# A transformer block stack on one core: the convolved x of the state-space mixer returns to token layout through 32x32 squares and DRAM instead of TensorE transposes, and the decay tiles are loaded later

## The chip, the cores and the metric

The kernel runs on one core of a Trainium2 chip. TensorE multiplies matrices, VectorE and ScalarE work element by element, GpSimd does very little here, and SyncE (SP) issues most of the transfers; ScalarE issues some on a queue of its own. Each engine works through its own instructions in a fixed order and stops at one whose inputs are not ready. The metric is device time in microseconds (us).

## What is computed

The input is 256 tokens of 2048 numbers. The first block is a hybrid mixer (a Mamba-2 style state-space branch, "SSD", and gated linear attention) with an MLP; two attention layers follow. Everything is float32. The change lies in the SSD branch:

```
z, xbc, dt, ... = split(h @ w_in)
xbc = silu(conv4(xbc) + b)                 # 4096 channels of x, 1024 of B, 1024 of C
x   = xbc's x as (256 tokens, 64 heads, 64)        # 8 groups g of 8 heads
xdt = x * dt
y_diag = einsum(cb * decay, xdt)           # decay = exp(masked differences of cumsum(dt*A))
states = einsum(B, xdt * exp(a_last - a_cs))
y   = y_diag + C @ states_before * exp(a_cs) + D * x
y   = grouped_rms_norm(y * silu(z)) ; branch = y @ w_ssd_branch
```

## The kernel before

**Products.** Each weight block of 128x1024 is a unit. SP loads it (`stage`, L128, tile `ws`, five buffers), ScalarE casts it to a rounded high part (L136, `wh`), VectorE subtracts to get the low part (L137, `wl`; five buffers each), and TensorE does three products per matrix (L141 high by high, L142 low by high, L143 high by low), twelve matmuls per unit. A unit can be cast only when TensorE has finished the unit five places ahead.

**Order.** `drive()` walks through the units; after every second unit it steps the generators ("posts") that treat finished products. The order on each engine is then settled by a scheduler when the program is built. `yield` marks where a post can be interrupted.

**One group of SSD.** For each of eight groups there are a product for x (512 channels), one for z, and from the third group on products of the w_ssd branch. `x_post` (L586) loads two decay tiles `E` of 128x1024 (one per half of the tokens) from `acs_rows` in DRAM, convolves, and then needs x by tokens: eight 128x128 transposes on TensorE (L603) into PSUM, multiplied by VectorE (L604 `xdt`, L607 `xw`, L609 `y`). ScalarE turns E into decays (eight relus L613 and one exp L615 per half), VectorE multiplies by `cbm` (L616). TensorE then does `st` (L620, copied by ScalarE at L622), `y` (L626, eight matmuls per half) and `yo` (L632). `z_post` (L638) multiplies y by silu(z), normalizes it and calls `to_op_t` (L359, L362), which makes the operand `yT` of the w_ssd branch.

**Turning through DRAM.** The convolution and `to_op_t` already use `turn`: VectorE transposes 32x32 squares (L328), ScalarE's queue writes them to a DRAM tile in four transfers of 128 KB (L334), and SP reads it back as one of 512 KB into `tn` (L337). SP and ScalarE stop in that order until the data is there. The DRAM tile `turn` has four buffers.

Of the kernel before, what the change touches and what calls it, by code (L numbers as in the profile page):

```python
# [13 lines left out]
ALU = mybir.AluOpType  # L14
# [3 lines left out]
P = 128  # L18
# [3 lines left out]
NB = 512  # L22
# [6 lines left out]
Z0, XBC0, DT0, Q0, K0, V0, G0, LR0, GS0, GG0 = (  # L29
    0, 4096, 10240, 10304, 11328, 12352, 14400, 16448, 16464, 18512)  # L30
# [23 lines left out]
W_IN_COLS = (  # L54
    [XBC0 + 4096 + 512 * i for i in range(4)]
    + [c for g in range(8) for c in (XBC0 + 512 * g, Z0 + 512 * g)]
    + [GS0 + 512 * i for i in range(4)]
    + [V0, V0 + 512, Q0, K0, V0 + 1024, V0 + 1536, Q0 + 512, K0 + 512]
    + [G0 + 512 * i for i in range(4)]
    + [GG0 + 512 * i for i in range(4)]  # L60
)
# [17 lines left out]
def tile_blocks(ctx, tc, a, out):  # L79
    nc = tc.nc  # L80
# [11 lines left out]
    def nm(s):  # L92
        uid[0] += 1
        return f"{s}_{uid[0]}"

    def t4(shape, dt=F32, s="t4"):
        return tpool.tile(shape, dt, tag="t4", name=nm(s))
# [4 lines left out]
    def small(shape, s="sm"):  # L102
        return spool.tile(shape, F32, tag="sm", name=nm(s))
# [4 lines left out]
    def aux(shape, s="aux"):  # L108
        return psa.tile(shape, F32, tag="aux", name=nm(s))
# [212 lines left out]
    def turn(src, got):  # L322

        sq = t4([P, 4, 4, 2, 32], s="sq")
        for m in range(2):
            V.transpose(sq[:, :, :, m, :].rearrange("p b c i -> p c b i"),  # L328
                        src[m].rearrange("p (c b j) -> p c b j", c=4, b=4))
        d = dram.tile([P, 1024], F32, tag="turn", name=nm("turn"), bufs=4)  # L330
        sv = sq.rearrange("p b c m i -> p (b c m i)")
        dv = d.rearrange("(b j) (q r) -> q j b r", b=4, q=4)
        for q in range(4):
            S.dma_start(dv[q], sv[32 * q:32 * q + 32, :].rearrange("j (b r) -> j b r", b=4))  # L334
        yield
        tn = t4([P, 4, 4, 2, 32], s="tn")
        nc.sync.dma_start(tn.rearrange("p q c m i -> p (q c m i)"), d)  # L337
        got.append(tn)
        yield
# [91 lines left out]
    ident = cst[:, C_ID:C_ID + P]  # L431
# [149 lines left out]
    def heads8(ap):  # L581
        return ap.rearrange("p (h d) -> p h d", h=8)
# [2 lines left out]

    def x_post(g, need):  # L586
        def post(ps):
            es = [t4([P, 8, P], s="E") for _ in range(2)]
            for m in range(2):
                nc.sync.dma_start(es[m], acs_rows[g, m].partition_broadcast(P))  # L590
            xc = t4([P, 4, T], s="xc")
            yield from conv_silu(ps, 4 * g, xc)
            for h in need:
                while not h[0].done:
                    yield
            hs = slice(8 * g, 8 * g + 8)
            y = ys[g] = t4([P, 2, 512], s="y")
            xdt = t4([P, 2, 512], s="xdt")
            xw = small([P, 512], "xw")
            for m in range(2):  # L600
                pt = aux([P, 512], "tr")
                for f in range(4):
                    nc.tensor.transpose(pt[:, f * P:f * P + P], xc[:, f, m * P:m * P + P], ident)  # L603
                V.tensor_tensor(heads8(xdt[:, m, :]), heads8(pt),  # L604
                                dt[:, m, hs].unsqueeze(2).to_broadcast([P, 8, 64]), op=ALU.mult)
                if m == 0:
                    V.tensor_tensor(heads8(xw), heads8(pt),  # L607
                                    dtw[:, hs].unsqueeze(2).to_broadcast([P, 8, 64]), op=ALU.mult)
                V.tensor_tensor(heads8(y[:, m, :]), heads8(pt),  # L609
                                Dbc[:, hs].unsqueeze(2).to_broadcast([P, 8, 64]), op=ALU.mult)  # L610
                e = es[m]
                for h in range(8):
                    S.activation(e[:, h, :], e[:, h, :], AF.Relu, scale=-1.0,  # L613
                                 bias=acs[:, m, 8 * g + h:8 * g + h + 1])
                S.activation(e, e, AF.Exp, scale=-1.0)  # L615
                V.tensor_tensor(e, e, cbm[m][:, g, :].unsqueeze(1).to_broadcast([P, 8, P]), op=ALU.mult)  # L616
                yield

            ps = aux([P, 512], "st")
            nc.tensor.matmul(ps, Btok[:, g, :], xw, start=True, stop=True)  # L620
            st = small([P, 512], "st")
            S.copy(st, ps)  # L622
            for m in range(2):
                py = aux([P, 512], "y")
                for h in range(8):
                    nc.tensor.matmul(py[:, h * 64:h * 64 + 64], es[m][:, h, :], xdt[:, m, h * 64:h * 64 + 64],  # L626
                                     start=True, stop=True)
                V.tensor_tensor(y[:, m, :], y[:, m, :], py, op=ALU.add)
                if m == 0:
                    yield  # L630
            po = aux([P, 512], "yo")
            nc.tensor.matmul(po, CT1[:, g, :], st, start=True, stop=True)  # L632
            yo = small([P, 512], "yo")
            V.tensor_tensor(heads8(yo), heads8(po), ea1[:, hs].unsqueeze(2).to_broadcast([P, 8, 64]),
                            op=ALU.mult)
            V.tensor_tensor(y[:, 1, :], y[:, 1, :], yo, op=ALU.add)
        return post
# [828 lines left out]
def _blocks(w, kcs=4, n=NB):  # L1466

    k, c = w.shape
    v = w.reshape(k // (kcs * P), kcs, P, c // n, n)
    return np.ascontiguousarray(v.transpose(3, 0, 2, 1, 4)).reshape(-1, P, kcs * n)  # L1470
# [29 lines left out]
def _vec(v):  # L1500

    return np.asarray(v).reshape(-1, P).T


def _bias(rpb):

    t = np.arange(T)
    r, c = t // 64, t % 64
    c0 = np.clip(c - 8, 0, 48)
    q, k = t[:, None], t[None, :]  # L1510
    inside = (c[k] >= c0[q]) & (c[k] < c0[q] + 16)
    dr = r[k] - r[q] + 7
    dc = np.where(inside, c[k] - c[q] + 15, 0)
    out = np.full((2, 4, T, T), -1e30, np.float32)
    out[:, :, inside] = rpb[:, :, dr, dc][:, :, inside]
    return np.ascontiguousarray(out.reshape(2, 4, 2, P, T).transpose(0, 1, 3, 2, 4)).reshape(2, 4, P, -1)


def _layout(x):
# [2 lines left out]
    o["x"] = a["x"][0]  # L1522
    o["xT"] = np.ascontiguousarray(a["x"][0].T.reshape(16, P, T).transpose(1, 0, 2)).reshape(P, 16 * T)
    o["consts"] = _consts()
    cw = a["ssd_conv_w"][0]
    o["vec"] = np.ascontiguousarray(np.concatenate(
        [_vec(cw[j]) for j in range(4)]
        + [_vec(a["ssd_conv_b"][0]), _vec(a["ssd_norm_w"][0]), _vec(a["gla_norm_w"][0]),
           _vec(a["ln1_g"][0]), _vec(a["ln1_b"][0]),
           _vec(a["ln2_g"][0]), _vec(a["ln2_b"][0]), _vec(a["norm_pre_2"][0]), _vec(a["norm_pre_2"][1]),  # L1530
           _vec(a["b_q_norm_2"][0]), _vec(a["b_q_norm_2"][1]), _vec(a["b_kv_norm_2"][0]),
           _vec(a["b_kv_norm_2"][1])], axis=1))
    w = a["w_in"][0]
    o["w_in"] = np.concatenate([_blocks(w[:, c:c + NB]) for c in W_IN_COLS])
    o["w_dtlr"] = _blocks(np.concatenate([w[:, LR0:LR0 + 16], w[:, DT0:DT0 + 64]], axis=1), 16, 80)[0]
    o["gk_w"] = np.concatenate([a["gla_gk_w"][0], a["gla_gk_b"]], axis=0)
    o["w_ssd"] = _blocks(a["w_ssd_branch"][0])
# [36 lines left out]
```

## Time and profile before

| | us |
|---|---|
| median of 3 runs | 2867.42 (2863.65 to 2869.07) |
| the profiled execution | 2869.14 |
| its span, first to last instruction | 2867.4 |
| TensorE busy in the span | 2835.7 (99%) |
| VectorE busy | 1816.3 (63%) |
| ScalarE busy | 1428.6 (50%) |

The granted TensorE clock averages 0.998 of full speed. The transfers move 603 MB, 210 GB/s over the span. The eight SSD groups lie between about 140 and 650 us. In a row of a timeline the first number is the start and the second the length, both in us; in square brackets stands how long the engine was idle before, and what released it. Engine names with a q (ACTq, SPq) are instructions that only issue a transfer. Lengths of matmuls overlap, so the pitch is read from their starts.

### The profile page before, as it was taken

What the parts mean: (1) busy time and instruction counts of PE and PEld (TensorE: products, weight loads), DVE (VectorE), ACT (ScalarE), POOL (GpSimd) and SP (SyncE); (2) the same over time, 40 slices, a digit from 0 to 9 for tenths busy, and PEclk for the clock granted to TensorE, in tenths of its full rate; (3) what the DMA queues carried; (4) which work ended last, traced back from release to release, by engine and by line L of the source; (5) the groups of instructions that cost most, each with busy time, mean ns of one, the idle gap of its engine ahead of it and who ended that gap; (6) DMA issues with size and microseconds to landing.
All of it is one profiled execution on the core that took longest, in us unless ns stands there. A gap on an engine that the chain in (4) does not pass through costs nothing.

```text
span 2867.4 us, 35163 instructions
## 1 busy us (share of the span) xinstructions
PE 2835.7 (99%) x13040; PEld 2343.8 (82%) x13040; DVE 1816.3 (63%) x2357; ACT 1428.6 (50%) x2013; POOL 37.8 (1%) x49
## 2 busy tenths in 40 slices
PE   9999999999999999999999999999999999999998
PEld 7787888888887878887888888888788888798887
DVE  6777677775844845665666555555776555666564
ACT  5565655554444544444444443444565544655543
POOL 0000000000000000000000000000000000000000
PEclk9999999999999999999999999999999999999999
DMA  8766666666664656675676666667466676466674
GB/s 287 220 218 216 220 221 220 221 221 214 189 183 141 216 159 224 216 270 163 218 233 223 222 213 216 210 223 253 149 199 221 195 233 221 147 212 215 215 236 140
DMA packets 199759, 603.15 MB, mean 210 GB/s; under 512 B 22545, under 2 KB 56721, under 8 KB 199586
## 3 DMA queue, kind: packets, MB, share of 16 engines
q1 hardware_dynamic: 161858, 566.27, 60.9%
q10 hardware_dynamic: 37728, 34.62, 3.9%
q8 instruction: 102, 1.67, 0.2%
q14 instruction: 71, 0.58, 0.1%
HBM read 564.56 MB, written 36.24 MB: 210 GB/s over the span
## 4 chain that ended last, share of the span: by engine, by line
PE 84%; DMA 7%; DVE 4%; ACT 2%; issue 1%; ACTq 1%; SPq 0%; DVEq 0%; POOL 0%; POOLq 0%
PE mm L141 26%; PE mm L142 26%; PE mm L143 26%; DMA turn<-sq 3%; DVE wl L137 2%; PE sc L1107 1%; DMA tn<-turn 1%; PE po L1139 1%; DMA ws<-in_w_in 1%; ACT wh L136 1%; DMA E<-acs_rows 1%; ACTq L334 1%; PE y L626 1%; PE tr L272 1%; ACT E L613 0%
## 5 line engine op out<-in xcount | busy, mean ns | idle before, releaser
L137 DVE TENSOR_TENSOR wl<-ws,wh 128x1024 fp32r<-128x1024 f32 (+2 forms) x974 | 1170.4, 1211 | 773.9 <-ACT wh L136 767.8
L136 ACT CAST wh<-ws 128x1024 fp32r<-128x1024 f32 (+2 forms) x974 | 1007.3, 1044 | 1006.6 <-PE mm L143 864.2
L141 PE MATMUL mm<-wh,xh 128*128 128x512 f32 x1280 | 503.9, 395 | 1.5 <-DVE xh L419 1.0
L142 PE MATMUL mm<-wl,xh 128*128 128x512 f32 x1280 | 499.1, 390 | 2.5 <-DVE wl L137 2.5
L143 PE MATMUL mm<-wh,xl 128*128 128x512 f32 x1280 | 499.0, 390 | 0.0
L141 PE MATMUL mm<-wh,lnh 128*128 128x512 f32 (+1 forms) x896 | 344.6, 388 | 6.0 <-ACT lnh L304 6.0
L142 PE MATMUL mm<-wl,lnh 128*128 128x512 f32 (+1 forms) x896 | 347.1, 387 | 0.0
L143 PE MATMUL mm<-wh,lnl 128*128 128x512 f32 (+1 forms) x896 | 346.4, 387 | 0.0
L141 PEld LDWEIGHTS mm<-wh,xh 128*128 128x128 f32 x1280 | 240.5, 188 | 56.8 <-issue 3.9
L142 PEld LDWEIGHTS mm<-wl,xh 128*128 128x128 f32 x1280 | 240.5, 188 | 55.9 <-DVE wl L137 4.5
L143 PEld LDWEIGHTS mm<-wh,xl 128*128 128x128 f32 x1280 | 240.3, 188 | 50.4 <-DVE xl L420 0.2
L141 PEld LDWEIGHTS mm<-wh,lnh 128*128 128x128 f32 x896 | 168.2, 188 | 40.2 <-ACT lnh L304 7.0
L142 PE MATMUL mm<-wl,hT 128*128 128x512 f32 x512 | 199.4, 389 | 0.5 <-DVE wl L137 0.5
L143 PE MATMUL mm<-wh,hT 128*128 128x512 f32 x512 | 199.2, 389 | 0.0
L141 PE MATMUL mm<-wh,hT 128*128 128x512 f32 x512 | 199.2, 389 | 0.0
L143 PEld LDWEIGHTS mm<-wh,lnl 128*128 128x128 f32 x896 | 168.2, 188 | 34.1 <-DVE lnl L305 0.9
L142 PEld LDWEIGHTS mm<-wl,lnh 128*128 128x128 f32 x896 | 168.2, 188 | 33.6 <-DVE wl L137 0.4
L141 PE MATMUL mm<-wh,hh 128*128 128x512 f32 (+1 forms) x384 | 147.7, 386 | 3.7 <-ACT hh L304 3.7
L142 PE MATMUL mm<-wl,hh 128*128 128x512 f32 (+1 forms) x384 | 148.0, 385 | 0.2 <-DVE wl L137 0.2
L143 PE MATMUL mm<-wh,hl 128*128 128x512 f32 (+1 forms) x384 | 147.3, 384 | 0.4 <-DVE hl L305 0.4
L142 PEld LDWEIGHTS mm<-wl,hT 128*128 128x128 f32 x512 | 96.1, 188 | 21.1 <-DVE wl L137 1.2
L141 PEld LDWEIGHTS mm<-wh,hT 128*128 128x128 f32 x512 | 96.1, 188 | 20.0
(371 smaller groups left out, 3408.3 us busy)
## 6 DMA issues: line engine op xcount, KB each, us to landing
ws<-in_w_in SPq DMA_DIRECT2D x494, 512.0 KB
ws<-in_w_up SPq DMA_DIRECT2D x128, 512.0 KB
ws<-in_w_down SPq DMA_DIRECT2D x128, 512.0 KB
ws<-in_w_out SPq DMA_DIRECT2D x96, 512.0 KB
turn<-sq ACTq DMA_DIRECT2D x260, 128.0 KB
tn<-turn SPq DMA_DIRECT2D x65, 512.0 KB
ws<-in_w_ssd SPq DMA_DIRECT2D x64, 512.0 KB
ws<-in_w_gla SPq DMA_DIRECT2D x32, 512.0 KB
```

Of the source, the lines that this page charges most:

```text
L136: S.copy(hi[:, c], st[:, c])
L137: V.tensor_tensor(lo[:, c], st[:, c], f32(hi[:, c]), op=ALU.subtract)
L141: nc.tensor.matmul(ps, l[0], r[0], start=first, stop=False)
L142: nc.tensor.matmul(ps, l[0], r[1], start=False, stop=False)
L143: nc.tensor.matmul(ps, l[1], r[0], start=False, stop=last)
L272: nc.tensor.transpose(dst[:, i, m * P:m * P + P], src[:, m, (ft + i) * P:(ft + i + 1) * P], ident)
L334: S.dma_start(dv[q], sv[32 * q:32 * q + 32, :].rearrange("j (b r) -> j b r", b=4))
L626: nc.tensor.matmul(py[:, h * 64:h * 64 + 64], es[m][:, h, :], xdt[:, m, h * 64:h * 64 + 64], start=True, stop=True)
L1107: nc.tensor.matmul(ps[:, m, :], l, rr, start=n == 0, stop=n == len(lr) - 1)
L1139: nc.tensor.matmul(po[:, m, :], pT[:, 2 * i + k, m * P:m * P + P], vals(h, k), start=k == 0, stop=k == 1)
```

## The change

`turn` is cut in two: the squares stay, and the trip through DRAM becomes `regroup`, which any squares can use. In `x_post` the eight transposes and their PSUM tiles go. VectorE makes squares of the convolved x (two instructions), `regroup` writes and reads them, and the five multiplies read `tn` in SBUF with a head as 2 x 64 columns of it. For that the host lays out the x columns of `w_in`, the convolution weights and bias in exchanged quarters (`_quarters`). The two E tiles are allocated, and their loads issued, after `regroup` instead of at the start of the post. New lines: L332 `regroup` (L338 writes, L341 read), L601 squares, L608 E loads, L614 multiplies, L626 relu, L628 exp, L629 `cbm`, L633 `st`, L635 its copy, L639 `y`, L645 `yo`.

```diff
--- before.py
+++ after.py
@@ -327,13 +327,17 @@
         for m in range(2):
             V.transpose(sq[:, :, :, m, :].rearrange("p b c i -> p c b i"),
                         src[m].rearrange("p (c b j) -> p c b j", c=4, b=4))
+        yield from regroup(sq, got)
+
+    def regroup(sq, got):
+
         d = dram.tile([P, 1024], F32, tag="turn", name=nm("turn"), bufs=4)
         sv = sq.rearrange("p b c m i -> p (b c m i)")
         dv = d.rearrange("(b j) (q r) -> q j b r", b=4, q=4)
         for q in range(4):
             S.dma_start(dv[q], sv[32 * q:32 * q + 32, :].rearrange("j (b r) -> j b r", b=4))
         yield
-        tn = t4([P, 4, 4, 2, 32], s="tn")
+        tn = t4(list(sq.shape), s="tn")
         nc.sync.dma_start(tn.rearrange("p q c m i -> p (q c m i)"), d)
         got.append(tn)
         yield
@@ -585,29 +589,38 @@
 
     def x_post(g, need):
         def post(ps):
-            es = [t4([P, 8, P], s="E") for _ in range(2)]
-            for m in range(2):
-                nc.sync.dma_start(es[m], acs_rows[g, m].partition_broadcast(P))
             xc = t4([P, 4, T], s="xc")
             yield from conv_silu(ps, 4 * g, xc)
             for h in need:
                 while not h[0].done:
                     yield
             hs = slice(8 * g, 8 * g + 8)
+
+            sq = t4([P, 4, 2, 4, 32], s="sq")
+            for m in range(2):
+                V.transpose(sq[:, :, m].rearrange("p a f j -> p f a j"),
+                            xc[:, :, m * P:m * P + P].rearrange("p f (a i) -> p f a i", a=4))
+            got = []
+            yield from regroup(sq, got)
+            xt = got[0].rearrange("p b m f j -> p b m (f j)")
+            es = [t4([P, 8, P], s="E") for _ in range(2)]
+            for m in range(2):
+                nc.sync.dma_start(es[m], acs_rows[g, m].partition_broadcast(P))
             y = ys[g] = t4([P, 2, 512], s="y")
             xdt = t4([P, 2, 512], s="xdt")
             xw = small([P, 512], "xw")
-            for m in range(2):
-                pt = aux([P, 512], "tr")
-                for f in range(4):
-                    nc.tensor.transpose(pt[:, f * P:f * P + P], xc[:, f, m * P:m * P + P], ident)
-                V.tensor_tensor(heads8(xdt[:, m, :]), heads8(pt),
-                                dt[:, m, hs].unsqueeze(2).to_broadcast([P, 8, 64]), op=ALU.mult)
+
+            def by_head(dst, m, w):
+                V.tensor_tensor(dst.rearrange("p (b s d) -> p b s d", b=4, s=2),
+                                xt[:, :, m, :].rearrange("p b (s d) -> p b s d", s=2),
+                                w.rearrange("p (b s) -> p b s", b=4).unsqueeze(3).to_broadcast([P, 4, 2, 64]),
+                                op=ALU.mult)
+
+            for m in range(2):
+                by_head(xdt[:, m, :], m, dt[:, m, hs])
                 if m == 0:
-                    V.tensor_tensor(heads8(xw), heads8(pt),
-                                    dtw[:, hs].unsqueeze(2).to_broadcast([P, 8, 64]), op=ALU.mult)
-                V.tensor_tensor(heads8(y[:, m, :]), heads8(pt),
-                                Dbc[:, hs].unsqueeze(2).to_broadcast([P, 8, 64]), op=ALU.mult)
+                    by_head(xw, m, dtw[:, hs])
+                by_head(y[:, m, :], m, Dbc[:, hs])
                 e = es[m]
                 for h in range(8):
                     S.activation(e[:, h, :], e[:, h, :], AF.Relu, scale=-1.0,
@@ -1502,6 +1515,11 @@
     return np.asarray(v).reshape(-1, P).T
 
 
+def _quarters(w):
+
+    return w.reshape(w.shape[0], -1, 4, 4, 32).transpose(0, 1, 3, 2, 4).reshape(w.shape)
+
+
 def _bias(rpb):
 
     t = np.arange(T)
@@ -1522,16 +1540,19 @@
     o["x"] = a["x"][0]
     o["xT"] = np.ascontiguousarray(a["x"][0].T.reshape(16, P, T).transpose(1, 0, 2)).reshape(P, 16 * T)
     o["consts"] = _consts()
-    cw = a["ssd_conv_w"][0]
+
+    cw, cb = (np.concatenate([_quarters(v[:, :4096]), v[:, 4096:]], axis=1)
+              for v in (a["ssd_conv_w"][0], a["ssd_conv_b"]))
     o["vec"] = np.ascontiguousarray(np.concatenate(
         [_vec(cw[j]) for j in range(4)]
-        + [_vec(a["ssd_conv_b"][0]), _vec(a["ssd_norm_w"][0]), _vec(a["gla_norm_w"][0]),
+        + [_vec(cb[0]), _vec(a["ssd_norm_w"][0]), _vec(a["gla_norm_w"][0]),
            _vec(a["ln1_g"][0]), _vec(a["ln1_b"][0]),
            _vec(a["ln2_g"][0]), _vec(a["ln2_b"][0]), _vec(a["norm_pre_2"][0]), _vec(a["norm_pre_2"][1]),
            _vec(a["b_q_norm_2"][0]), _vec(a["b_q_norm_2"][1]), _vec(a["b_kv_norm_2"][0]),
            _vec(a["b_kv_norm_2"][1])], axis=1))
     w = a["w_in"][0]
-    o["w_in"] = np.concatenate([_blocks(w[:, c:c + NB]) for c in W_IN_COLS])
+    o["w_in"] = np.concatenate([_blocks(_quarters(w[:, c:c + NB]) if XBC0 <= c < XBC0 + 4096 else w[:, c:c + NB])
+                                for c in W_IN_COLS])
     o["w_dtlr"] = _blocks(np.concatenate([w[:, LR0:LR0 + 16], w[:, DT0:DT0 + 64]], axis=1), 16, 80)[0]
     o["gk_w"] = np.concatenate([a["gla_gk_w"][0], a["gla_gk_b"]], axis=0)
     o["w_ssd"] = _blocks(a["w_ssd_branch"][0])
```

The third group (g = 2) is shown on three engines. On TensorE, before, `st` and the first half of `y` stand inside the w_ssd products of `mm_2424`, and the second half and `yo` 22 matmuls later:

```order
L141 MATMUL mm_2424<-wh_2362,yT_1647 128x512
L142 MATMUL mm_2424<-wl_2363,yT_1647 128x512
L620 MATMUL st_2456<-xw_2343,Btok 128x512
L626 MATMUL y_2460<-xdt_2342,E_2088 128x64 x8
L143 MATMUL mm_2424<-wh_2362,yT_1647 128x512
...
L142 MATMUL mm_2425<-wl_2381,yT_1647 128x512
L143 MATMUL mm_2425<-wh_2380,yT_1647 128x512
L626 MATMUL y_2506<-xdt_2342,E_2089 128x64 x8
L632 MATMUL yo_2516<-st_2458,CT_43_109 128x512
L141 MATMUL mm_2543<-wh_2418,xh_81 128x512
```

After, on TensorE, `st` is followed by 34 matmuls, and then both halves of `y` and `yo` stand together:

```order
L143 MATMUL mm_2425<-wh_2385,yT_1732 128x512
L141 MATMUL mm_2543<-wh_2418,xh_81 128x512
L633 MATMUL st_2456<-xw_2353,Btok 128x512
L142 MATMUL mm_2543<-wl_2419,xh_81 128x512
L143 MATMUL mm_2543<-wh_2418,xl_82 128x512
...
L141 MATMUL mm_2544<-wh_2470,xh_81 128x512
L142 MATMUL mm_2544<-wl_2471,xh_81 128x512
L639 MATMUL y_2460<-xdt_2352,E_2347 128x64 x8
L639 MATMUL y_2506<-xdt_2352,E_2348 128x64 x8
L645 MATMUL yo_2516<-st_2458,CT_43_109 128x512
L143 MATMUL mm_2544<-wh_2470,xl_82 128x512
```

`st` moved 23 matmuls back and the first `y` 57, counted in matmuls of products from the start of the program (1082 to 1105, 1082 to 1139).

On ScalarE, before, the decay tiles of the third group (`E_2088`, `E_2089`) are made beside the state copy of the group before it:

```order
L136 CAST wh_1975<-ws_1831 128x1024
L136 CAST wh_1993<-ws_1867 128x1024
L613 ACTIVATE E_2088<-E_2088,acs_98 128x128 x8
L136 CAST wh_2025<-ws_1887 128x1024
L613 ACTIVATE E_2089<-E_2089,acs_98 128x128 x8
L615 ACTIVATE E_2088<-E_2088 128x1024
L622 COPY st_2013<-st_2011 128x512
L615 ACTIVATE E_2089<-E_2089 128x1024
L382 ACTIVATE junk_86,yss_2076<-y_1901 128x512
```

After, on ScalarE, the tiles of the same group (`E_2347`, `E_2348`) stand behind the writes of the new trip (`turn_2308`), three casts and two copies:

```order
L136 CAST wh_2385<-ws_2235 128x1024
L338 DMA turn_2308<-sq_2305 32x4x256 x4
L136 CAST wh_2418<-ws_2253 128x1024
L136 CAST wh_2438<-ws_2291 128x1024
L684 COPY acc_2415<-mm_2315 128x512
L684 COPY acc_2415<-mm_2316 128x512
L136 CAST wh_2470<-ws_2333 128x1024
L626 ACTIVATE E_2347<-E_2347,acs_98 128x128 x8
L626 ACTIVATE E_2348<-E_2348,acs_98 128x128 x8
L136 CAST wh_2488<-ws_2371 128x1024
L628 ACTIVATE E_2347<-E_2347 128x1024
L684 COPY acc_2534<-mm_2424 128x512
```

The relus are now a group later in the program and behind the trip of their own group.

On SP, after, the read-backs of the z trip (`tn_2267`) and of the x trip (`tn_2313`) and the E loads stand among the weight loads:

```order
L341 DMA tn_2267<-turn_2215 128x1024
L128 DMA ws_2291<-in_w_in 128x1024
L128 DMA ws_2333<-in_w_in 128x1024
L128 DMA ws_2371<-in_w_in 128x1024
L128 DMA ws_2389<-in_w_in 128x1024
L341 DMA tn_2313<-turn_2308 128x1024
L608 DMA E_2347<-acs_rows 128x1024
L608 DMA E_2348<-acs_rows 128x1024
L128 DMA ws_2422<-in_w_in 128x1024
```

Before, the two E loads stood between weight loads with no read-back ahead of them at that place:

```order
L128 DMA ws_1926<-in_w_in 128x1024
L128 DMA ws_1944<-in_w_in 128x1024
L590 DMA E_2088<-acs_rows 128x1024
L590 DMA E_2089<-acs_rows 128x1024
L128 DMA ws_1979<-in_w_in 128x1024
L128 DMA ws_1997<-in_w_in 128x1024
L128 DMA ws_2029<-in_w_in 128x1024
```

The E loads moved to right behind the new read-back.

## Rows read from the trace of the kernel before

**Rows 1.** The page: busy time of each engine, and the two costliest groups of instructions

```profile
PE 2835.7 (99%) x13040; PEld 2343.8 (82%) x13040; DVE 1816.3 (63%) x2357; ACT 1428.6 (50%) x2013; POOL 37.8 (1%) x49
...
L137 DVE TENSOR_TENSOR wl<-ws,wh 128x1024 fp32r<-128x1024 f32 (+2 forms) x974 | 1170.4, 1211 | 773.9 <-ACT wh L136 767.8
L136 ACT CAST wh<-ws 128x1024 fp32r<-128x1024 f32 (+2 forms) x974 | 1007.3, 1044 | 1006.6 <-PE mm L143 864.2
```

**Rows 2.** Timeline of TensorE: start, length, line, instruction, [idle before, releaser], both in us

```profile
150.99 0.50 PE L142 MATMUL mm<-wl,xh 128*128 128x512 f32 x1 [1.15 <-DVE wl L137]
...
233.42 2.05 PE L632 MATMUL yo<-st,CT 128*128 128x512 f32 x2 [2.65 <-ACT st L622]
```

**Rows 3.** Stretches of 2 us: busy time by engine, granted clock, DMA share, GB/s

```profile
234.00:236.00 2.00, 2.00 (x4) 0.97 (x3) 2.00 (x4) 2.00 (x5) 0.00 (x0) 0.50 0.03 12
236.00:238.00 2.00, 2.00 (x8) 1.56 (x8) 2.00 (x3) 0.82 (x1) 0.00 (x0) 0.78 0.25 59
```

**Rows 4.** Timeline of TensorE at the first four transposes of group 0, and the step after

```profile
159.06 0.60 PE L603 MATMUL tr<-cst,xc 128*128 128x128 f32 x4
...
159.73 0.40 PE L142 MATMUL mm<-wl,xh 128*128 128x512 f32 x1
```

**Rows 5.** Timeline of TensorE: group 0's st, y and yo, with 21 matmuls between

```profile
170.91 1.02 PE L620 MATMUL st<-xw,Btok 128*128 128x512 f32 x2
171.76 1.89 PE L626 MATMUL y<-xdt,E 128*128 128x64 f32 x16
...
174.25 0.39 PE L141 MATMUL mm<-wh,xh 128*128 128x512 f32 x1
...
179.03 1.89 PE L626 MATMUL y<-xdt,E 128*128 128x64 f32 x16
180.76 1.08 PE L632 MATMUL yo<-st,CT 128*128 128x512 f32 x2
```

**Rows 6.** Timeline of ScalarE in one round trip of z and one load of E

```profile
436.04 2.25 ACTq L334 DMA_DIRECT2D turn<-sq  x4
...
446.58 1.71 ACT L359 ACTIVATE yT<-tn,vec 128x256 fp32r<-128x256 f32 x4 [2.58 <-DMA tn<-turn]
...
450.38 2.45 ACT L613 ACTIVATE E<-E,acs 128x128 f32<-128x128 f32 x8 [1.15 <-DMA E<-acs_rows]
```

**Rows 7.** Timeline of SP: read-back of the same trip, and of a shorter one

```profile
388.16 0.33 SPq L337 DMA_DIRECT2D tn<-turn  x1
...
443.02 0.33 SPq L337 DMA_DIRECT2D tn<-turn  x1
```

**Rows 8.** Timeline of ScalarE: the longest and the shortest of the trips read

```profile
193.00 1.78 ACTq L334 DMA_DIRECT2D turn<-sq  x4
...
205.60 1.71 ACT L359 ACTIVATE yT<-tn,vec 128x256 fp32r<-128x256 f32 x4 [2.12 <-DMA tn<-turn]
...
383.10 0.31 ACTq L334 DMA_DIRECT2D turn<-sq  x1
...
392.12 1.14 ACT L531 COPY u<-tn 128x512 f32<-128x512 f32 x2 [1.10 <-DMA tn<-turn]
```

**Rows 9.** By tile: count, minimum, median and maximum ns, first and last start

```profile
L615 ACT ACTIVATE E<-E x16: 1039/1052/1066, 131.9 to 602.3; 128x1024 f32<-128x1024 f32 x16
L616 DVE TENSOR_TENSOR E<-E,cbm x16: 1181/1219/1226, 133.0 to 603.9; 128x1024 f32<-128x1024 f32 x16
...
L328 DVE STREAM_TRANSPOSE sq<-y x16: 668/687/705, 191.7 to 650.8; 128x512 f32<-128x512 f32 x16
```

**Rows 10.** Timeline of VectorE: end of group 0's convolution

```profile
156.05 0.69 DVE L546 SCALAR_TENSOR_TENSOR xc<-cth,xc 128x512 f32<-128x512 f32 x1
```

**Rows 11.** Timeline of ScalarE: decay tiles of group 1, and the tanh of a z

```profile
169.75 4.20 ACT L613 ACTIVATE E<-E,acs 128x128 f32<-128x128 f32 x14 [6.22 <-DMA E<-acs_rows]
...
211.54 1.07 ACT L386 ACTIVATE th<-mm 128x512 f32<-128x512 f32 x2
```

**Rows 12.** Stretch of the groups' first part: busy time by engine, clock, DMA share

```profile
140.00:300.00 160.00, 156.21 (x730) 128.04 (x729) 118.30 (x170) 93.94 (x150) 2.11 (x3) 0.99 0.67 215
```

## Prediction

> **What bounds the kernel now.** I read the page first, then the timelines of each engine through the eight groups, then single tiles. On the page the reader is to see TensorE busy 99% of the span, and the two engines that prepare its weights idle most often for it: ScalarE's casts were idle 1006.6 us, 864.2 of it for TensorE [rows 1]. So time is won only where TensorE has less to do or waits less, and lost wherever it waits for something new. The timeline of TensorE shows what it does wait for among the groups: 1.15 us for a low weight part and 2.65 us for a state copy [rows 2]. Behind the second of these the granted clock is 0.50 and 0.78 in two stretches of 2 us, between full speed and the lower of its two levels (2.4 and 1.2 GHz) [rows 3]: a wait of this length costs a further 2 x (0.50 + 0.22) = 1.4 us. The pitch of a product matmul is (179.03 - 174.25)/21 = 0.228 us [rows 5].
>
> The profiled execution took 2869.14 us, with a span of 2867.4, and lies 1.7 us above the median of the runs, 2867.42. Differences are worked out in its rows and added to the median.
>
> **What goes.** Four transposes and one product step take 159.73 - 159.06 = 0.67 us [rows 4]; less the step's 0.228 they cost 0.44, and there are sixteen such fours: -7.1 us. The two waits also go, -3.8, with the clock behind the longer, -1.4. The wait for the low part came while VectorE and ScalarE did early E work beside the convolution of group 0, and that work now stands later. The wait for the state copy stood just behind a `y`; now `st` stands 34 matmuls ahead of `yo` in the third group, so its copy is long done. Together -12.3 us.
>
> **What comes without a wait of its own.** Sixteen squares of 0.69 us [rows 9] are 11 us of VectorE, and 32 issues of writes at 2.25/4 = 0.56 us [rows 6] are 18 us of ScalarE, over a stage in which they are busy 118 and 94 of 160 us in its first part [rows 12]. Cost 0 while the five casts ahead hold; where ScalarE stands still for long, this cover is gone (third rival). The 8 MB more of traffic are small beside the 215 GB/s in this stretch, 0.67 of the transfer engines' time [rows 12], but every trip must queue among it. The multiplies from SBUF instead of PSUM are not seen in this shape; between no change and twice the 0.7 us of a 128x512 square [rows 9] I take no change, the shape and type being the same.
>
> **The new chain.** The two trips and the E loads now lie in a row. For one trip of this form, from the first write's issue to `yT`, 446.58 - 436.04 = 10.5 us [rows 6]; the shortest read is 392.12 - 383.10 = 9.0 and the longest 205.60 - 193.00 = 12.6 [rows 8]. From the read-back's issue on SP to E's first relu it is 450.38 - 443.02 = 7.4 us [rows 6, 7], and from first write to the read-back 443.02 - 436.04 = 7.0, or 388.16 - 383.10 = 5.1 in the short one [rows 6 to 8]. So E is there 14.3 us after the first write of x (12.4 with the short leg, 16.4 with the 2.1 us more of the longest trip). That the E loads stood there one weight load behind the read-back, and now directly behind it, leaves this leg as it is. Behind it ScalarE does eight relus twice, 2 x 2.45 [rows 6], a cast 1.04 [rows 1], an exp 1.05, and VectorE one multiply 1.22 [rows 9]: 8.2 us until the first `y` can run.
>
> Third group. The cast ahead of its z writes (`wh_2287`) waits for matmul 1008, which frees its buffer. From there 1.04 for the cast, 10.5 for the z trip, then `yT` 1.7, two tanhs of z 1.1 and one of the convolution 0.5 [rows 11], on VectorE the last half of sz 0.7 (the shape in [rows 10]) and the squares 1.4 [rows 9]: 5.4 in all; then 14.3 and 8.2. Sum 39.4 us. TensorE needs for the 131 matmuls up to `y` 29.8 and for `st` 0.85 [rows 5], 30.7 us. Wait 8.7. The second `y` then needs two copies 1.1 (as the pair in [rows 8]), a cast 1.04 and an exp 1.05, less the first half's 180.76 - 179.03 = 1.7 [rows 5]: 1.5. Together 10.2 (6.8 to 14.4 by the ends of the two legs). Part may be paid earlier, at the first product with the new `yT`; the sum is then the same.
>
> Second group. From matmul 792: cast 1.04, four convolution steps 1.7 (the shape of `yT`), 10.5, 5.4 and one low part 1.2, 14.3, 8.2 and two write issues 1.1, in all 43.4, against 183 matmuls and `st`, 42.5: 0.9. The second half adds two issues 1.1, a copy 0.6, a cast and an exp, less 1.7: 2.1. Together 3.0 (0.5 to 7.2).
>
> First group. Here a cast (`wh_1520`) stands behind fifteen relus of E. The convolution ends at 156.05 + 0.69 [rows 10]; sz 0.7 and squares 1.4 give 158.8; + 14.3 + 15 x 0.3 [rows 11] + 1.04 + 1.21 = 179.9 us. TensorE stands at the place of the old transposes at 159.06 - 1.15 = 157.9 and needs 85 matmuls, 19.4: 177.3. Wait 2.6 (0.7 to 4.7).
>
> From the fourth group on, 288 matmuls instead of 192 belong to a group, and the same chain is nearly covered: 0.5 (0 to 6).
>
> The waits are 10.2 + 3.0 + 2.6 + 0.5 = 16.3 (8.0 to 32.3). Behind the third group's and one more the clock falls as in [rows 3]: 2 x 1.4 = 2.8 (1.4 to 4.2).
>
> **The sum.** -12.3 + 16.3 + 2.8 = +6.8 us. On the median: 2874.2. With all low ends it is -12.3 + 8.0 + 1.4 = -2.9; with all high ends, and the low part's wait of 1.15 left where it is, -11.1 + 32.3 + 4.2 = +25.4.
>
> Two rules of the Trainium skill bear on this; nothing above rests on them. The trace shows four transposes at 0.44 us of TensorE against 1.4 us of squares on VectorE and a trip of 10.5 us [rows 4, 6, 9]. "VectorE: DVE Perf Modes", section Rules for kernel authors, says to give a full 128x128 transpose to TensorE where the result may go to PSUM, and to VectorE only squares of 32; by this rule the way back to tokens was on the right engine before. The trace agrees on latency and disagrees on TensorE's time, where the change saves. The trip is the other point: 7.0 us pass from the first write's issue to the read-back's, for 512 KB [rows 6, 7]. "DMA: Bandwidth & Descriptors", section Anatomy of one DMA, gives for the GpSimd path about 2 us plus the bytes at 436 GB/s; an estimate by it is 3.2 us for 512 KB, so 6.4 for a trip and 9.6 with E. By it the two legs are 4.1 and 4.7 us shorter and the third group's 8.7 us goes, which is the first rival; the trips in the rows are all longer than this.
>
> **Rivals.** *Covered (faster).* All trips are as short as the third group needs: 8.7 us less over its two legs. For it: a trip queues behind weights, and where these leave more of the transfer engines' other third [rows 12] it gets shorter. Against it: the short ends together give only 3.4 us. What goes stays, -12.3, second halves and one clock fall cost 2 to 4: about 2858.
>
> *Balance (no change).* The legs come out near their short ends, waits and clock cost 8 to 16 in sum: between 2863 and 2871, say 2868. For it: the short trip was read in this stage; against it: two of three trips were longer, and the x trip of the second group shares the queue with others.
>
> *Standing still (slower still).* ScalarE waits in order at `yT` and E, and VectorE at the multiplies on `tn`. Behind E's relus in the third group stand the casts `wh_2488` and `wh_2537`; behind the multiplies on VectorE the low part of `wh_2470`. If a wait lasts longer than the five units ahead, 5 x 12 x 0.228 = 13.7 us, TensorE also waits for weights, in this and the next group, at 2.3 us (cast and low part) per late unit and with a lower clock. SP stops at the read-backs, too, so loads come late. It decides from a leg of 16 us on; six late units and two more clock falls give 13.5 + 2.8 above the forecast: about 2890. For it: the casts stood behind waits for `tn` of 2.58 and 2.12 us already [rows 6, 8]; against it: both stayed short of the cover.
>
> That the change does not do what it says is excluded: the transposes are gone from TensorE's order, and `y` has moved behind the trip.
>
> **How the numbers follow.** Forecast 0.43, covered 0.20, balance 0.20, standing still 0.17. This kernel's measurement tells a difference of 0.2%, 5.7 us, from none. The forecast's own spread (2868 to 2882) lies two thirds above 2873.1 and one third within; balance is within; so faster 0.20, same 0.33, slower 0.47. The range goes from 2857 to 2890: below lies a part of the covered case, above half of standing still.
>
> **What would show it.** Right: the first `y` of the third group idles 7 to 14 us, released by VectorE's E multiply (L629), with a clock near half behind it; E's relu (L626) waits for its load; no transposes stand in the stage, and the fourth group on shows no wait over 3 us. The casts of the five units ahead stay on time. Wrong: E there within 9 us of the first x write (covered), or TensorE idling for casts or low parts over 5 us in a group (standing still). What would upset the whole sum is a loss outside 140 to 650 us, where the order is unchanged.

## The result, and the profile after

The changed kernel took 2886.25 us (median of 4 runs, 2884.31 to 2890.54) against 2865.76 of the kernel before: a ratio of 1.0071, 95% interval 1.0059 to 1.0084, or 20 us more. The profiled execution took 2884.97 us, 15.8 more than that of before, which lies above its median while this one lies below; the span rose from 2867.4 to 2883.1.

The page of the changed kernel has TensorE with 64 instructions fewer and yet busier, since matmuls take longer at the lower clock shown below, and the two engines that prepare weights nearly as they were:

```profile
span 2883.1 us, 35101 instructions
PE 2838.5 (98%) x12976; PEld 2344.5 (81%) x12976; DVE 1824.2 (63%) x2373; ACT 1427.1 (49%) x2013; POOL 37.2 (1%) x49
```

Beside [rows 1], VectorE is up by 8 us, not by the 11 of the squares alone. Where the time went is seen from one group of matmuls that spans the SSD stage, those on `yT`, in the last two numbers before the semicolon (first and last start). Before:

```profile
L143 PE MATMUL mm<-wh,yT x256: 387/389/476, 258.3 to 777.0; 128*128 128x512 f32 x128
```

After:

```profile
L143 PE MATMUL mm<-wh,yT x256: 388/389/628, 263.7 to 793.7; 128*128 128x512 f32 x128
```

The last of them starts 16.7 us later, and the span is 15.7 longer: the loss lies ahead of it, in the stage that was changed. What TensorE waited for there, in its timeline after (start, length, instruction, idle before and releaser):

```profile
177.74 0.50 PE L142 MATMUL mm<-wl,xh 128*128 128x512 f32 x1 [2.32 <-DVE wl L137]
183.09 0.50 PE L142 MATMUL mm<-wl,xh 128*128 128x512 f32 x1 [0.74 <-DVE wl L137]
224.43 0.50 PE L141 MATMUL mm<-wh,xh 128*128 128x512 f32 x1 [0.53 <-ACT wh L136]
225.97 0.50 PE L142 MATMUL mm<-wl,xh 128*128 128x512 f32 x1 [1.04 <-DVE wl L137]
240.00 1.22 PE L633 MATMUL st<-xw,Btok 128*128 128x512 f32 x1 [3.07 <-DVE xw L614]
274.85 0.79 PE L141 MATMUL mm<-wh,yT 128*128 128x512 f32 x1 [6.03 <-ACT yT L363]
448.16 0.47 PE L639 MATMUL y<-xdt,E 128*128 128x64 f32 x1 [2.94 <-DVE E L629]
665.24 0.32 PE L639 MATMUL y<-xdt,E 128*128 128x64 f32 x1 [0.98 <-DVE E L629]
```

The 1.15 us at 150.99 of [rows 2] is now 0.84 at 153.35, and the 2.65 for the state copy is gone. With the small ones, all waits between 80 and 700 us are 20.6 us, against 6.4 before: 13.0 at `st`, `yT` and `y`, 5.7 for weight parts, and 1.9 others. Behind the long ones the clock fell. In stretches of 2 us (the third number from the end is PEclk, then DMA share and GB/s):

```profile
240.00:242.00 2.00, 2.00 (x3) 0.96 (x4) 2.00 (x4) 0.33 (x2) 0.00 (x0) 0.50 0.96 358
242.00:244.00 2.00, 2.00 (x8) 1.62 (x7) 2.00 (x3) 2.00 (x8) 0.00 (x0) 0.75 1.03 420
...
274.00:276.00 2.00, 1.15 (x3) 0.96 (x4) 1.17 (x5) 1.71 (x5) 0.00 (x0) 0.50 1.02 324
276.00:278.00 2.00, 2.00 (x6) 1.52 (x5) 2.00 (x6) 1.47 (x3) 0.00 (x0) 0.50 0.83 332
278.00:280.00 2.00, 2.00 (x6) 1.61 (x5) 2.00 (x4) 0.00 (x0) 0.00 (x0) 0.50 0.04 16
280.00:282.00 2.00, 2.00 (x9) 1.55 (x9) 0.04 (x1) 1.00 (x1) 0.00 (x0) 0.86 0.05 12
...
448.00:450.00 2.00, 1.84 (x9) 1.84 (x9) 2.00 (x3) 2.00 (x3) 0.00 (x0) 0.50 0.73 248
450.00:452.00 2.00, 2.00 (x10) 2.00 (x10) 2.00 (x3) 1.87 (x3) 0.00 (x0) 0.50 0.77 227
452.00:454.00 2.00, 2.00 (x6) 1.52 (x6) 2.00 (x3) 0.00 (x0) 0.00 (x0) 0.50 0.68 186
454.00:456.00 2.00, 2.00 (x10) 1.62 (x9) 1.07 (x2) 0.72 (x2) 0.00 (x0) 0.84 0.86 326
```

Busy time of TensorE times the missing share of the clock gives 1.5, 2.9 and 3.2 us for these three, and 1.7 for the one behind the wait at 177.74: 9.3 us, where the whole stage before had the one fall of [rows 3], 1.5 with the stretch ahead of those rows.

The trips themselves are in ScalarE's timeline after, from the first write of x to the first relu of E, in groups 0, 1, 2 and 4:

```profile
161.32 0.31 ACTq L338 DMA_DIRECT2D turn<-sq  x1
...
176.35 4.49 ACT L626 ACTIVATE E<-E,acs 128x128 f32<-128x128 f32 x15 [9.41 <-DMA E<-acs_rows]
...
227.16 2.04 ACTq L338 DMA_DIRECT2D turn<-sq  x4
...
241.67 0.69 ACT L626 ACTIVATE E<-E,acs 128x128 f32<-128x128 f32 x2 [6.53 <-DMA E<-acs_rows]
...
281.06 1.78 ACTq L338 DMA_DIRECT2D turn<-sq  x4
...
292.17 4.79 ACT L626 ACTIVATE E<-E,acs 128x128 f32<-128x128 f32 x16 [2.35 <-DMA E<-acs_rows]
...
423.70 2.15 ACTq L338 DMA_DIRECT2D turn<-sq  x4
...
439.98 0.40 ACT L626 ACTIVATE E<-E,acs 128x128 f32<-128x128 f32 x1 [8.35 <-DMA E<-acs_rows]
```

They are 15.0, 14.5, 11.1 and 16.3 us long, against the 14.3 put together from [rows 6, 7]; in groups 3, 5, 6 and 7 they are 13.4, 13.7, 15.0 and 14.7. The third group's is by far the shortest, and its `y` did not wait at all:

```profile
302.80 3.68 PE L639 MATMUL y<-xdt,E 128*128 128x64 f32 x32
```

In the first group fifteen relus stand ahead of a cast, as the prediction had it, but only the 0.74 us at 183.09 follows from that place. The 2.32 us at 177.74 ended when the low part at 176.47 was made, and that one stood on VectorE behind the five multiplies on `tn`, for which VectorE had waited 6.01 us; its cast had been done since 166.95. VectorE after, with the low part behind the multiplies and the one behind the relus' cast:

```profile
173.45 0.69 DVE L614 TENSOR_TENSOR xdt<-tn,dt 128x512 f32<-128x512 f32 x1 [6.01 <-DMA tn<-turn]
...
176.47 1.22 DVE L137 TENSOR_TENSOR wl<-ws,wh 128x1024 fp32r<-128x1024 f32 x1
181.81 1.22 DVE L137 TENSOR_TENSOR wl<-ws,wh 128x1024 fp32r<-128x1024 f32 x1 [4.12 <-ACT wh L136]
```

### The profile page after: what moved, and what is told of

Its sections match the earlier page's. It is cut to its first block, busy times and chain, and to the rows that moved or that the text cites. A ratio compares the mean times of both kernels' runs of the same rounds, so it can differ in the third digit from the quotient of the medians.

```text
span 2883.1 us, 35101 instructions
## 1 busy us (share of the span) xinstructions
PE 2838.5 (98%) x12976; PEld 2344.5 (81%) x12976; DVE 1824.2 (63%) x2373; ACT 1427.1 (49%) x2013; POOL 37.2 (1%) x49
## 4 chain that ended last, share of the span: by engine, by line
PE 79%; DMA 8%; DVE 6%; ACT 4%; issue 2%; ACTq 1%; SPq 0%; POOL 0%; DVEq 0%; POOLq 0%
PE mm L143 24%; PE mm L141 24%; PE mm L142 24%; DMA turn<-sq 4%; DVE wl L137 2%; DMA tn<-turn 2%; ACT wh L136 1%; PE sc L1120 1%; DMA E<-acs_rows 1%; PE po L1152 1%; ACTq L338 1%; ACT E L626 1%; PE y L639 1%; DMA ws<-in_w_in 1%; PE tr L272 1%
## 5 line engine op out<-in xcount | busy, mean ns | idle before, releaser
L141 PEld LDWEIGHTS mm<-wh,hT 128*128 128x128 f32 x512 | 96.1, 188 | 20.0
L143 PEld LDWEIGHTS mm<-wh,hT 128*128 128x128 f32 x512 | 96.1, 188 | 19.9
```

The source lines that it names most:

```text
L141: nc.tensor.matmul(ps, l[0], r[0], start=first, stop=False)
L143: nc.tensor.matmul(ps, l[1], r[0], start=False, stop=last)
```

## The experiments

Each was timed beside the kernel before on the same chip; ratios are to that. In the first table two things vary: how x gets to tokens, and whether E is loaded ahead of the convolution (early) or behind it, in the changed kernel behind the trip (late). The trip also brings two interruptions of the post with it, which are taken up further down, and with "neither" x stays by channels, so those two kernels compute another y.

| | early E | late E |
|---|---|---|
| TensorE's transposes | 1 (kernel before) | 1.0060 (1.0048 to 1.0072) |
| squares and trip | 1.0052 (1.0040 to 1.0064) | 1.0071 (the change) |
| neither | 0.9981 (0.9972 to 0.9989) | 1.0045 (1.0031 to 1.0059) |

**Trip, early E.**

```diff
         def post(ps):
+            es = [t4([P, 8, P], s="E") for _ in range(2)]
+            for m in range(2):
+                nc.sync.dma_start(es[m], acs_rows[g, m].partition_broadcast(P))
             xc = t4([P, 4, T], s="xc")
...
             xt = got[0].rearrange("p b m f j -> p b m (f j)")
-            es = [t4([P, 8, P], s="E") for _ in range(2)]
-            for m in range(2):
-                nc.sync.dma_start(es[m], acs_rows[g, m].partition_broadcast(P))
```

> The changed kernel with one thing undone: the two E loads of a group are issued at the start of its post again, ahead of the convolution; squares and trip stay. Theory E (the late decay tiles carry the loss): in the changed kernel the weight waits of 2.32 and 0.74 us behind E's relus, the 2.94 and 0.98 us at y, and the late y that makes yT late (6.03 us) all hang on E; without them and the clock falls behind them the time is 2858 to 2870, within 0.3% of the kernel before (ratio 0.997 to 1.002). Theory T (the trip itself carries it): xw and yT still come late, only the 2.94 and 0.98 us at y go; 2875 to 2884 (ratio 1.003 to 1.006).

1.0052: theory E, as the only cause, falls. No wait for E is left at `y`, but others have grown; two of them, in TensorE's timeline of this kernel:

```profile
272.90 0.79 PE L141 MATMUL mm<-wh,yT 128*128 128x512 f32 x1 [7.17 <-ACT yT L363]
...
425.56 0.50 PE L141 MATMUL mm<-wh,yT 128*128 128x512 f32 x1 [2.63 <-DVE sz L391]
```

**Transposes, late E.**

```diff
         def post(ps):
-            es = [t4([P, 8, P], s="E") for _ in range(2)]
-            for m in range(2):
-                nc.sync.dma_start(es[m], acs_rows[g, m].partition_broadcast(P))
...
+            es = [t4([P, 8, P], s="E") for _ in range(2)]
+            for m in range(2):
+                nc.sync.dma_start(es[m], acs_rows[g, m].partition_broadcast(P))
             hs = slice(8 * g, 8 * g + 8)
```

> The kernel before with one thing moved: TensorE keeps its transposes, but the E loads are issued after the convolution, ahead of the transposes. Theory E: from the load's issue E needs 7.4 us to arrive and 8.2 more until y, 15.6 against the 13 us from the convolution's end to y in the kernel before, so some of the loss is here already: +4 to +10 us (ratio 1.0015 to 1.0035). Theory T: the slack covers it, -2 to +2 us.

1.0060, 17 us: beyond both. The waits at `y` are short (1.02, 0.71 and 1.11 us). More is lost for weight parts, 9.5 us in all; the longest are 1.99 at 478.90, 1.99 at 555.04 and 1.59 at 630.21, each with its casts behind a stand of ScalarE of 6.0 to 7.0 us at the convolution's read-back. One wait of either kind:

```profile
478.90 0.50 PE L142 MATMUL mm<-wl,yT 128*128 128x512 f32 x1 [1.99 <-DVE wl L137]
...
498.52 0.32 PE L626 MATMUL y<-xdt,E 128*128 128x64 f32 x1 [1.11 <-DVE E L616]
```

Its waits in the stage rose by 6.3 us in all and the clock's share by 3.6. At the last matmul on `yT` the trace is 14.2 us late, so some 4 us of it are in neither; what they are stays open.

**Neither, early E; neither, late E.**

```diff
-            sq = t4([P, 4, 2, 4, 32], s="sq")
...
-            yield from regroup(sq, got)
-            xt = got[0].rearrange("p b m f j -> p b m (f j)")
+            xt = xc.rearrange("p b (m t) -> p b m t", m=2)
```

> Early E loads, and neither transposes nor squares nor trip: the five multiplies read the convolved x where it lies, by channels, so x is not brought to tokens and y is another one. What the removed transposes are worth with nothing in their place: -7.1 us by the prediction's term, up to -13 with the two old waits and their clock gone (ratio 0.9955 to 0.9975). Both theories agree; if the ratio is above 0.999, the term for the transposes was wrong.

> Late E loads (issued after the convolution), and neither transposes nor squares nor trip: the multiplies read the convolved x by channels, so x is not brought to tokens and y is another one. It completes the table of what the E loads' place costs: +17 us beside the transposes, about +2 beside the trip. Theory A (E's own chain of load, relu, exp, multiply sets y): +12 to +18 on the 2862 of the same kernel with early E, ratio 1.002 to 1.005. Theory B (E late hurts only because it meets other work, the transposes or the trip): within 4 us of 2862, ratio 0.997 to 0.9995.

Without anything in their place the transposes are worth 5.4 us by the ratio (3.2 to 8.0 by its interval). In the trace the last matmul on `yT` starts 8.5 us earlier than before:

```profile
L143 PE MATMUL mm<-wh,yT x256: 387/389/398, 250.6 to 768.5; 128*128 128x512 f32 x128
```

Late E costs 17 to 18 us here too, though nothing else stands between convolution and `y`, as theory A gave it: E's own chain holds up `y`, with 8.9 of the 13.5 us of waits there. For example, with late E:

```profile
420.52 0.32 PE L633 MATMUL y<-xdt,E 128*128 128x64 f32 x1 [2.19 <-DVE E L623]
```

So each half of the change by itself costs 15 to 17 us against the kernel before, and both together 20, not 32. That both hold up the same `y` would explain it; no run separates that from other causes.

**The trip unused; two interruptions.** In the first the squares and the trip were added to the kernel before, with the transposes left to do the work. The second has only this:

```diff
                     yield
+            yield
+            yield
             hs = slice(8 * g, 8 * g + 8)
```

> The kernel before, with the squares and the trip through DRAM added but their result unused: TensorE's transposes still bring x to tokens, E loads early. Left is what the trip costs by being there: 11 us of VectorE, 18 us of issues on ScalarE, SP standing at the read-back, 8 MB of traffic. Prediction's term: 0 (ratio 0.999 to 1.0015). Theory T, in the form that standing queues carry the loss: +5 us or more (ratio above 1.0015).

> The kernel before with nothing added but two bare interruptions (yield) between the convolution and the transposes, as many as the trip has: no squares, no transfers, early E. They move st and y of each group 24 to 48 product matmuls later in TensorE's order, to 744, 936, 1084, 1416 and so on, as in the kernel with the unused trip (744, 936, 1106, 1416). Theory P (the place of y in the order, hence a late yT, is what the trip costs even without anybody waiting for it): the wait for yT at the first w_ssd product shows, some 6 us with 3 us of clock; +4 to +9 us, ratio 1.0015 to 1.003, as the unused trip's 1.003. Theory W (the trip's own work, issues and traffic): -2 to +2 us.

1.0030 (1.0020 to 1.0041) and 1.0016 (1.0007 to 1.0025). The unused trip costs 9 us although no matmul needs what it brings. Two bare interruptions alone cost 5: `drive()` steps a post once in 24 matmuls, so they put `y` up to 48 matmuls later, and `yT` is late at its first use. With the unused trip, and with two interruptions, that wait is:

```profile
262.76 0.80 PE L141 MATMUL mm<-wh,yT 128*128 128x512 f32 x1 [5.97 <-ACT yT L363]
```

```profile
260.29 0.50 PE L141 MATMUL mm<-wh,yT 128*128 128x512 f32 x1 [2.40 <-ACT yT L359]
```

The prediction's nought for squares, issues and traffic is therefore neither borne out nor refuted: what is left beside the interruptions is some 4 us by the middle values, and the intervals overlap. What it left out is that the steps of the post have a place in the order.

**Another queue.** Writes and read-back of x's trip on GpSimd, or the read-back alone, with early E.

```diff
-            yield from regroup(sq, got)
+            yield from regroup(sq, got, G, G)
```

The two last arguments are the engines that issue writes and read-back; for the read-back alone they are `None, G`.

> Trip and early E loads, and the four writes and the read-back of x's trip issued on GpSimd's queue, so that neither ScalarE issues them nor SP stands at the read-back. Theory Q (standing queues: SP's weight loads and the z trip wait behind the x trip): most of the 15 us over the kernel before goes, ratio 0.998 to 1.002. Theory V (VectorE stands in order at the multiplies on tn, so low parts and sz come late, and y and yT with it): TensorE still waits for sz and yT, ratio 1.0035 to 1.006.

> Trip and early E loads, with the read-back of x's trip alone issued on GpSimd's queue; ScalarE issues the writes as before. If SP's standing is the part of theory Q that counts, the ratio is that of the kernel with both on GpSimd (within 0.1%); if ScalarE's 18 us of issues count, it stays near 1.005 while the other falls.

1.0088 (1.0074 to 1.0102) and 1.0129 (1.0115 to 1.0143): neither is better than 1.0052, so theory Q's ratio does not come. That standing queues cost nothing is not shown by it, since the trip grew as well. With both on GpSimd it took 16.4, 14.8 and 12.9 us in groups 0 to 2 from the first write to the first multiply, against 11.3, 11.8 and 11.0 with early E alone. Group 0's, and the wait for `yT`, 8.45 us:

```profile
159.23 2.37 POOL L338 DMA_DIRECT2D turn<-sq  x4 [158.33 <-DVE sq L604]
...
175.59 0.69 DVE L614 TENSOR_TENSOR xdt<-tn,dt 128x512 f32<-128x512 f32 x1 [9.36 <-DMA tn<-turn]
...
270.98 0.79 PE L141 MATMUL mm<-wh,yT 128*128 128x512 f32 x1 [8.45 <-ACT yT L363]
```

**Multiplies a step later**, with early E.

```diff
             yield from regroup(sq, got)
+            yield
```

> Trip and early E loads, with one more interruption between the read-back and the multiplies, so that the multiplies on tn stand about two units later in VectorE's order. Theory V: VectorE no longer stands, the waits for sz (10.3 us from the third group on, with their clock falls) go, ratio 0.999 to 1.003; the wait for yT may grow by up to 5 us, since y is later. Theory Q: no change, 1.004 to 1.006.

1.0110 (1.0096 to 1.0124): theory V's ratio does not come. The waits for sz from the fourth group on became waits for the tanh of z and an accumulation, of about 2 us each, and the wait for sz ahead of `yT` is 7.12 us. To put the steps later costs more here than to let VectorE stand; what VectorE's stand costs by itself is not separated by it.

**E between squares and trip.**

```diff
+            es = [t4([P, 8, P], s="E") for _ in range(2)]
+            for m in range(2):
+                nc.sync.dma_start(es[m], acs_rows[g, m].partition_broadcast(P))
             got = []
             yield from regroup(sq, got)
```

> The changed kernel with the E loads issued between the squares and the trip, so ahead of its read-back on SP and about 7 us earlier, but not beside the convolution. If E's own chain behind the read-back is what y waits for, the weight waits behind E's relus and the waits at y go and the ratio falls to 1.000 to 1.004; if the trip's latency for xw, y and yT sets the time whatever E does (as early E showed, 1.0052), it stays at 1.004 to 1.008.

1.0100 (1.0086 to 1.0114), outside both: worse than early and than late E. TensorE waits less for E and more for `xw` (2.20, 2.19 and 1.08 us at `st`). The order that the scheduler makes differs, and why this place is the worst stays open.

**Straight from SBUF to SBUF**, with early E.

```diff
-            yield from regroup(sq, got)
+            yield from across(sq, got)
...
+        for b in range(4):
+            for q in range(4):
+                (S if b < 2 else nc.sync).dma_start(tv[32 * b:32 * b + 32, q, :], sv[32 * q:32 * q + 32, b, :])
```

> Early E loads, and the trip of x without DRAM: sixteen transfers of 32 KB per group from the squares straight to their place in another SBUF tile, eight issued by ScalarE and eight by SP, instead of four writes and a read-back. Theory L (the trip's latency, two transfers one after the other with a queue between, is the cost): one leg falls away, some 5 us of 10, and the waits for xw, sz and yT shrink with it: ratio 0.997 to 1.002, against 1.0052 with the two legs. Against it: if the number of issues or the traffic counts, 1.004 to 1.010.

1.0041 (1.0029 to 1.0054) against 1.0052: the intervals overlap, so theory L is not shown. Nor is it refuted, because no leg of some 5 us fell away: from the first issue to the first multiply groups 0 to 2 took 12.9, 8.8 and 10.9 us, against 11.3, 11.8 and 11.0, and the eight issues on ScalarE alone took up to 7.4. There is no wait left at `st` or `y` in groups 0 to 2, where the trip through DRAM had 1.83 us for `xw`, but the wait for `yT` stands as before:

```profile
267.06 0.80 PE L141 MATMUL mm<-wh,yT 128*128 128x512 f32 x1 [7.68 <-ACT yT L374]
```

**w_ssd products later**, in the changed kernel.

```diff
-        for n in range(2 * (g % 2), 2 * (g % 2) + 2):
-            if q:
-                ssd_branch(q - 1, n, zh[2 * q - 2:2 * q])
+        for k in range(2 * g - 6, 2 * g - 4):
+            if k >= 0:
+                ssd_branch(k // 4, k % 4, zh[2 * (k // 4):2 * (k // 4) + 2])
+    for n in (2, 3):
+        ssd_branch(2, n, zh[4:6])
```

> The changed kernel with the w_ssd products two places later in the order of jobs (the first two from the fourth group on, the last two of that kind after the eighth), so that yT has a group more until its first use. Theory P: the wait for yT (6.03 us and 2.9 of clock) goes, ratio 1.003 to 1.005 against 1.0071. Against it: the third group has only 192 matmuls now to cover its trip, and waits of 3 us at st or y appear there: 1.006 to 1.009. A version faster than the kernel before is expected of neither.

1.0050 (1.0037 to 1.0062), the ratio that theory P gave, but not for its reason. The wait at the first product on the new `yT` did not go; it rose from 6.03 to 9.83 us, the last of it for sz, whose tanh stands behind `yT` on ScalarE:

```profile
331.05 0.79 PE L141 MATMUL mm<-wh,yT 128*128 128x512 f32 x1 [9.83 <-DVE sz L391]
```

What went are the wait of 2.94 us at `y` and one of the clock's four falls, 3.7 us of clock in all. No version was faster than the kernel before but the one that leaves the turning out.

## Why the prediction was right, and where its sizes were off

Slower was forecast, by 6.8 us; it was 20 by the medians and 16.7 in the trace at the end of the stage. The direction and the kind of loss were right: of the 20.6 us of waits, 13.0 are at `st`, `yT` and `y`, behind the trips. That the waits' sum came out and that the time lies in the range is in part luck, as the terms show. The point of departure for them is the kernel with neither transposes nor trip, with early E.

**What goes (-12.3).** That kernel gives -8.5 in the trace and -5.4 by the medians, so the term is mis-sized by some 4 us. The clock's fall went, and the 2.65 us for the state copy, but not the waits as a sum: they are 5.5 us there, against 6.4 before. Of the 1.15 for the low part 0.75 is left at 149.23, and others of 0.5 to 1.2 have come.

**The waits (16.3).** From the trace without transposes and trip, 5.5 us of waits in the stage, to the changed one, 20.6: 15.1. Right as a sum, but the groups don't follow the prediction. In the first the number came out (2.6 against 2.32 + 0.74) for another reason: the cast behind the relus, on which the 2.6 was worked out, gave 0.74, and VectorE's stand at `tn` gave 2.32. The second waited 4.6 instead of 3.0, 3.1 of it at `st` for `xw`, not at `y` for E, and 1.6 for weights whose casts stood behind `yT` on ScalarE. The third waited 6.0 instead of 10.2, at the first product on the second group's half of `yT`; the prediction named such a product as a place where part could be paid. The rest did not come, and both trips were at or under its short ends: the z trip 9.0 us (265.32 to 274.29), the leg to E 11.1 instead of 12.4 at the least. The sign that it named first, 7 to 14 us at the first `y` of this group, did not come. From the fourth group on it was 4.1 instead of 0.5, the largest at 448.16 behind a trip of 16.3 us, the length from which the third rival was said to decide.

**The clock (2.8).** This term failed most: 9.3 us. Two falls of 1.4 us were taken from the one in [rows 3]. There were four, and two of them were twice as long, three stretches at 0.50 each, one behind a wait of 6.03 us and one behind a wait of only 2.94.

The three together: -8.5 + 15.1 + 9.3 = 15.9, of 16.7 measured at that point. The leg of 14.3 lies within the 11.1 to 16.3 measured, and the chain behind it was right: 448.16 - 439.98 = 8.2 us from the first relu to `y`. What the sum did not see at all is the place of steps: an edit with two more interruptions shifts `y` even where nobody waits for data.

**Its reading of the page.** VectorE does not idle for TensorE there: 767.8 of the 773.9 us ahead of its low parts end with ScalarE's cast [rows 1]. Nothing in the sum hangs on it.

**The two rules of the Trainium skill.** The estimate of 6.4 us for a trip, by "DMA: Bandwidth & Descriptors", section Anatomy of one DMA, did not hold for any trip read here; the shortest are 9.0 us in the changed kernel (265.32 to 274.29) and 7.5 in the one with the w_ssd products later (332.83 to 340.30). The rule of "VectorE: DVE Perf Modes", section Rules for kernel authors, that gives a full transpose to TensorE, did hold: the transposes cost 5 to 9 us in this kernel, and each replacement tried made the kernel 12 us or more slower than before.

**The rivals.** *Covered* and *balance* did not come as times, but the short trip on which *covered* rests came in the very group that it names. Its writes began at 281.06, where 12 to 16 GB/s moved (278 to 282 us), and the read-back followed 3.7 us later instead of 7.0. TensorE had just stood for 6.03 us; that this emptied the queue fits, but no run tests it. Of *standing still* a small part came, the 2.32 us of the first group and the 1.7 of clock behind it. TensorE ran out of low parts 8.0 us after VectorE had finished its last one (167.44 to 175.42), where the prediction gave the units ahead 13.7 us.

## What to carry to other kernels

A handful of operations on a saturated engine can be cheaper than their replacement on idle ones, if the replacement lengthens a chain that ends at the saturated engine: sum the chain from the last place where it is tied to that engine, and give every longer wait that comes out a clock loss as well, as a range: the trace before had a single fall, of 1.5 us, and those after cost 1.5 to 3.2. Two halves of a change need not add (15 and 17 us gave 20 here); test them in a table of two by two or more. In a kernel whose side work advances in fixed steps of the main loop, a step more is itself a delay (5 us for two here). And engines that work in order pass a stand on: a read-back that VectorE waits for can starve TensorE of weights that have nothing to do with it.

## What the runs showed of the hardware

Behind a wait the granted clock stood at 0.50, the lower of its two levels (1.2 GHz), and how long does not follow the wait's length. After waits of 2.65 [rows 3] and 3.07 us it was one whole stretch of 2 us and parts of its neighbours; after one of 6.03 us, counting the end of the wait itself, and after one of 2.94 us it was three whole stretches. With early E a wait of 7.17 us was followed by a loss of only 1.45 us; the clock fell within the wait, to 0.74 at 268 to 270 us, and was back at 1.00 from 276 us. With x sent straight from SBUF to SBUF a wait of 1.93 us was followed by 5.1 us of loss, the largest found between 80 and 700 us in any trace here:

```profile
579.65 1.40 PE L644 MATMUL st<-xw,Btok 128*128 128x512 f32 x2 [1.93 <-DVE xw L625]
580.85 6.92 PE L650 MATMUL y<-xdt,E 128*128 128x64 f32 x32
...
582.00:584.00 2.00, 2.00 (x12) 2.00 (x11) 2.00 (x3) 0.62 (x1) 0.00 (x0) 0.50 0.42 109
...
588.00:590.00 2.00, 2.00 (x6) 1.52 (x6) 1.47 (x3) 0.00 (x0) 0.00 (x0) 0.50 0.81 256
```

Behind this wait, as behind the 2.94, TensorE ran `y` matmuls (128x64); behind the others it ran products, `st` or `yo`. Whether that is why no run tests.

The same trip issued on GpSimd's queue was longer (16.4, 14.8 and 12.9 us against 11.3, 11.8 and 11.0), and the kernel with the read-back alone there was 22 us slower (1.0129 against 1.0052) than with it on SP.
